# Feed-forward: weight places, the place of the last norm, and row additions moved from POOL to DVE

## The chip, the cores and the metric

The kernel runs on one core of a Trainium2 chip. The metric is the device time in microseconds of one execution, the median over runs. The engines named below: PE (TensorE, with its weight loads apart as PEld), DVE (VectorE), ACT (ScalarE), POOL (GpSimd) and SP (SyncE), whose queue issues all of this kernel's DMAs.

## What is computed

One layer of a streaming encoder for 1024 prompt tokens and 64 sample tokens with the same weights: attention with two groups of heads, cross-attention into a memory, then a feed-forward with a convolution. The change touches the end of the memory output projection and the feed-forward alone:

```python
def conv_ffn(h, prev, w_up, w_conv, b_conv, w_down):
    gu = h @ w_up
    gate, val = gu[..., :D_FF], gu[..., D_FF:]
    t = gate.shape[1]
    gp = jnp.concatenate([prev.astype(gate.dtype), gate], axis=1)
    conv = sum(gp[:, j:j + t] * w_conv[j] for j in range(CONV_W)) + b_conv
    y = (jax.nn.silu(conv) * val) @ w_down
    return y, gp[:, -(CONV_W - 1):]
...
xp = xp + mem_attend(rms_norm(xp, g_norm2[l]), mk, mv, w_mq[l], g_mq[l], w_mo[l])
f, conv_p = conv_ffn(rms_norm(xp, g_norm3[l]), zeros_prev, w_up[l], w_conv[l], b_conv[l], w_down[l])
xp = xp + f
```

D_MODEL is 1024 and D_FF 2816, all float32. The sample tokens go through the same code.

## The kernel before

Everything lies transposed: 128 features on the partitions, the 1088 tokens as columns, in two halves of H = 544 and four quarters of Q = 272. Each float32 operand of a matmul is split into a rounded part (`hi`, a cast on ACT) and the rest (`lo`, a subtraction on DVE), by `two_parts` (L1244 to L1246) or, with the norm's gain, `gained_parts` (L1248). A product of two such operands is three matmuls (`SPLIT`: hi hi, hi lo, lo hi).

**Order of the work.** The Python code traces the instructions in the order in which it runs. The framework's planner then gives each engine its queue: it simulates costs and can draw an instruction forward when it finds the engine free and the operands there. Each engine then runs its queue strictly in that order. SP's queue of DMAs is one of them.

**The end of the memory output.** The loop at L1409 makes the second half of the eight feature rows, in the order `ROWS` = 0, 4, 1, 5, 2, 6, 3, 7. `evict_mo` (L1230) adds the residual to the product on DVE (L1233), stores the row, squares it on ACT (L1241) and adds the square to `accs[1]` on POOL (L1242). `t_sums` (L1391 to L1404) makes the sums and differences of row blocks that the products of the up projection take on the right; it holds `vSh` and `vSl` as scratch.

**The up projection.** Both feed-forward matrix products are cut into 2 x 2 blocks and made with seven block products instead of eight, M1 to M7. Up: for each of 22 column tiles n (NF) the order is M1, M2, M6, M5, M7, M3, M4 (L1310). Each block product is 24 matmuls of 272 columns (`product`, L1371, the matmul at L1381) into one of four PSUM tiles `wides`. Its left operand is a quarter of the weights (n, 0 to 3), or a sum of quarters. `load_more` (L1332) loads quarters in order into the places of `raws`: two `kvraw`, then `vSh` and `vSl`, then three `raw` places of the stream of earlier weights. `prepare` (L1340) makes the sums on DVE (M6: L1348 and L1349; M7: L1351; M3: L1353) and splits the operand. The right operands are the parts that `t_sums` made, `t3_parts` (four splits, for M7) and `t4_parts` (four splits, for M4, in places that `accs[1]` and the sums held).

`norm3(z)` (L1288) sums `accs[z]` over the features with two matmuls of float32 (four in the trace, L1292) and makes 1/rms on DVE and ACT (L1295 to L1300). `rs[1]` is read by the gate's convolution (L1486), first after M3. `finish` (L1513) evicts a product; M1, M5 and M6 are kept aside on ACT (L1517). The loop around the change:

```python
for g, (n, what) in enumerate(order):
    hi_lo = ops.pop((n, what))
    w = product(n, what, ...)
    parts_.give(hi_lo)
    if g == 0:
        t3_parts()
        norm3(1)
        t4_parts()
    finish(n, what, w)
    while prepared < min(len(order), g + 1 + AHEAD):
        prepare(prepared)
        prepared += 1
```

**The down projection.** `DOWN` = M2, M1, M5, M3, M6, M7, M4 (L1549), each over 11 steps f, each step four row blocks m of six matmuls (L1678) into the same four PSUM tiles `ws`. `prepare_down` (L1595) makes the operands two steps ahead: sums on DVE (L1603, L1604 for M5; L1606, L1607 for M3; L1609 for M6; L1611, L1612 for M7; L1614 for M4) and two splits. At the last step of a product `finish_down` (L1626) adds each tile to the output row `y_of(k, z)` on DVE (through `add`, L1452). M5 and M6 start the tiles anew, so they must wait for that. M1's product belongs to four output blocks: ACT copies it to `p` (L1631), and its additions to two further rows (L1632, L1633) and the residual of the rows m + 4 (`residual`, L1639: a load of x into the one buffer `early_x` at L1642 and an addition at L1643) are put on the list `later`, of which one entry is taken after each step (L1689). All run on POOL.

Of the kernel before, what the change touches and what calls it, by code (L numbers as in the profile page):

```python
# [40 lines left out]
def hybrid_step(ctx: ExitStack, tc: tile.TileContext, i: dict, o: dict):  # L41
# [3 lines left out]
    def f32(ap):  # L45
        return ap.bitcast(F32)
# [1183 lines left out]
    def evict_mo(m, z, q0, q1, src, x):  # L1230

        x = x[:, q0:q1]
        dve.tensor_tensor(like(x, src), src, like(x, src), op=ALU.add)  # L1233
        nc.sync.dma_start(xd[m, :, z * H + q0:z * H + q1], x)
        if m == ROWS[0]:
            if accs[z] is None:
                accs[z] = long_row(("sq", "pth")[z])
            act.activation(accs[z][:, q0:q1], x, ACT.Square, scale=1.0 / 32)
        else:
            sq = long_row("qlo")[:, :q1 - q0]  # L1240
            act.activation(sq, x, ACT.Square, scale=1.0 / 32)  # L1241
            pool.tensor_tensor(accs[z][:, q0:q1], accs[z][:, q0:q1], sq, op=ALU.add)  # L1242

    def two_parts(hi, lo, t, e=None):  # L1244
        act.copy(hi, t)  # L1245
# [66 lines left out]
    def stream_place(tag):  # L1312
        return stream.pl.tile([P, 4, P], F32 if tag == "raw" else F32R, name=tag, bufs=3 if tag == "raw" else 4).rearrange("p k c -> p (k c)")

    def flat(tag):
        if tag in ("vSh", "vSl"):
            return pl.tile([P, 2, Q], F32R, name=tag).rearrange("p a b -> p (a b)")[:, :512]
        return tmp(tag, [P, 2, 256]).rearrange("p a b -> p (a b)")

    raws = Slots([lambda: f32(flat("kvraw"))] * 2 + [lambda x=x: f32(flat(x)) for x in ("vSh", "vSl")] + [lambda: stream_place("raw")] * 3)  # L1320
    parts_ = Slots([lambda x=x: (flat(x + "h"), flat(x + "l")) for x in ("kP", "vP", "kS")]
                   + [lambda: (stream_place("hi"), stream_place("lo"))] * 4)

# [210 lines left out]
    for g, (n, what) in enumerate(order):  # L1534
        hi_lo = ops.pop((n, what))
        w = product(n, what, lambda p, j: hi_lo[p][:, j * P:(j + 1) * P], 4, [right(what, j) for j in range(4)], True, True)
        parts_.give(hi_lo)
        if g == 0:
            t3_parts()
            norm3(1)  # L1540
            t4_parts()
        finish(n, what, w)
# [3 lines that stand above are left out]
# [9 lines left out]
    def y_of(m, z):  # L1555

        return tall[m + 8 * z]
# [68 lines left out]
    def finish_down(what, m, w):  # L1626
        k, z = {"M2": (m, 0), "M1": (m, 0), "M5": (m + 4, 1), "M3": (m, 1), "M6": (m, 1), "M7": (m + 4, 1), "M4": (m + 4, 0)}[what]
        dst = y_of(k, z)
        if what == "M1":
            p = y_of(m + 4, 0)  # L1630
            act.copy(halves(p), both(w))  # L1631
            later.extend([lambda: pool.tensor_tensor(y_of(m, 1), y_of(m, 1), p, op=ALU.add),  # L1632
                          lambda: pool.tensor_tensor(y_of(m + 4, 1), y_of(m + 4, 1), p, op=ALU.add)])  # L1633
            later.extend([lambda q=q: residual(m, q) for q in range(2)])
        add(dst, w, dst)
        if what in ("M1", "M6", "M7", "M4"):
            nc.sync.dma_start(o["yT"][k, :, z * H:z * H + H], dst)

    def residual(m, q):  # L1639

        c = slice(q * Q, q * Q + Q)
        nc.sync.dma_start(early_x[:, :Q], xd[m + 4, :, c])  # L1642
        pool.tensor_tensor(y_of(m + 4, 0)[:, c], y_of(m + 4, 0)[:, c], early_x[:, :Q], op=ALU.add)  # L1643

    later = []
    for f in range(NG):
        load_b("M2", f)
    load_a()
# [12 lines left out]
    for s, (what, f) in enumerate(steps):  # L1661
        if f < NG - 1:
            prepare_down(s + 2)
            load_a()
            nxt = DOWN.index(what) + 1
            if nxt < len(DOWN):
                load_b(DOWN[nxt], f)
                if f == NG - 2:
                    load_b(DOWN[nxt], NG - 1)
        if f == NG - 1:  # L1670
            continue
        for m in range(4):
            for x in ((s,) if f < NG - 2 else (s, s + 1)):
                la, ra = down_ops[x]
                first, final = steps[x][1] == 0, steps[x][1] == NG - 1
                for z in range(2):
                    for y, (p, b) in enumerate(SPLIT):
                        pe.matmul(ws[m][:, z, :Q], la[p][:, m * P:(m + 1) * P], ra[b][:, z * Q:z * Q + Q],  # L1678
                                  start=first and y == 0 and what in opening, stop=final and y == 2 and what in closing, skip_group_check=True)
            if f == NG - 2:  # L1680
                finish_down(what, m, ws[m])
        for x in ((s,) if f < NG - 2 else (s, s + 1)):
            la, ra = down_ops.pop(x)
            parts_.give(la)
            rights_.give(ra)
        if f == NG - 2:
            prepare_down(s + 3)
            load_a()
        if later:  # L1689
            later.pop(0)()  # L1690
    assert not later
    late_left.close()
    in_order(tc)

# [102 lines left out]
```

## Time and profile before

| | |
|---|---|
| Time, median of 3 runs | 1813.85 us (1813.5 to 1814.9) |
| The profiled execution's own time | 1811.59 us |
| Span of its trace, first to last instruction | 1809.8 us |
| Mean granted TensorE clock | 0.987 |
| Busy: PE, DVE, ACT, POOL | 1724.4, 1226.5, 929.6, 683.9 us |

The feed-forward runs from about 1091 us to the end: the up projection to 1562, the down projection to 1806. Busy times overlap, since the engines run beside each other. In a row of the timeline, what stands in brackets is the idle time of the engine before the instruction and what ended it; rows of like instructions are merged ("x2"), and since matmuls are pipelined, the busy times of neighbours overlap.

### The profile page before, as it was taken

Reading aid. Unit: us, or ns where it says so; the run is one execution under the profiler, and the core shown is the slowest. Engines: PE = TensorE matmul, PEld = TensorE weight load, DVE = VectorE, ACT = ScalarE, POOL = GpSimd, SP = SyncE. Lnnn points to the kernel's source line nnn. Section 1 sums busy time; section 2 is a strip of 40 time slices with the busy share of each in tenths; the row PEclk is TensorE's granted clock in tenths of the full one; section 3 lists DMA queues with packets and bytes.
Section 4 is the critical chain, followed back from the end, with each engine's and each line's share of the span. In section 5 each row is a group of like instructions: output and inputs, shape, how many; then the busy total and the mean of one; then the engine's idle time right before and its main releaser. Section 6 shows DMA issues by size and latency. Waiting matters only on the chain.

```text
span 1809.8 us, 34045 instructions
## 1 busy us (share of the span) xinstructions
PE 1724.4 (95%) x12412; PEld 1668.5 (92%) x12412; DVE 1226.5 (68%) x2693; ACT 929.6 (51%) x2042; POOL 683.9 (38%) x1042
## 2 busy tenths in 40 slices
PE   6899999999997898999999999999999999998999
PEld 5789999999997777999999998999999999998999
DVE  5777667677676788333444378877777777677974
ACT  5646666777676567334455455333333333433332
POOL 5746657878776454443343612000000001003000
PEclk9999999999998998999999999999999999999999
DMA  8312122122113767441111562222222222894222
GB/s 283 95 44 73 39 74 78 51 72 75 44 57 118 226 208 229 148 145 53 53 47 63 164 218 77 78 76 84 88 81 72 72 72 83 293 301 130 80 95 79
DMA packets 134104, 200.13 MB, mean 111 GB/s; under 512 B 20824, under 2 KB 73944, under 8 KB 133936
## 3 DMA queue, kind: packets, MB, share of 16 engines
q1 hardware_dynamic: 133936, 197.96, 34.5%
q8 instruction: 97, 1.59, 0.4%
q14 instruction: 71, 0.58, 0.1%
HBM read 155.61 MB, written 45.44 MB: 111 GB/s over the span
## 4 chain that ended last, share of the span: by engine, by line
PE 47%; DVE 4%; issue 1%; DMA 1%; POOL 1%; ACT 1%; SPq 0%; POOLq 0%; DVEq 0%; ACTq 0%
PE W L1381 25%; PE W L1678 9%; PE pj L869 7%; PE W L869 2%; PE S L1124 1%; PE tq L1160 1%; PE O L1160 1%; POOL lo L852 1%; DVE lo L1246 1%; DMA kvraw<-in_w_down_dram 0%; PE PT L1147 0%; DMA raw<-in_w_down_dram 0%; DVE f L1246 0%; PE O L1124 0%; DMA f<-x2d 0%
## 5 line engine op out<-in xcount | busy, mean ns | idle before, releaser
L272 PE MATMUL pj<-whi,xhi 128*128 128x384 f32 (+1 forms) x512 | 195.4, 382 | 7.9 <-ACT xhi L130 6.8
L272 PE MATMUL pj<-wlo,xhi 128*128 128x384 f32 (+1 forms) x512 | 177.1, 346 | 3.6 <-POOL wlo L123 3.3
L272 PE MATMUL pj<-whi,xlo 128*128 128x384 f32 (+1 forms) x512 | 175.4, 343 | 4.3 <-DVE xlo L131 4.3
L1487 POOL COPY s<-gp 128x2 f32<-128x2 f32 x22 | 15.8, 719 | 337.2 <-DVE gp L1486 337.2
L1678 PE MATMUL W<-f,hi 128*128 128x272 f32 x672 | 129.2, 289 | 7.7 <-DVE gp L1452 5.5
L458 ACT ACTIVATE s<-s,mx 128x640 f32<-128x640 f32 (+7 forms) x128 | 94.3, 736 | 80.0 <-DVE mx L456 78.3
L1381 PE MATMUL W<-h,hi 128*128 128x272 f32 x704 | 134.2, 288 | 0.7 <-ACT hi L1245 0.7
L495 DVE TENSOR_TENSOR ptl<-PT,pth 128x512 fp32r<-128x512 f32 (+2 forms) x192 | 99.5, 522 | 38.0 <-ACT pth L494 35.7
L1678 PEld LDWEIGHTS W<-f,hi 128*128 128x128 f32 x672 | 106.4, 190 | 8.8 <-DVE gp L1452 6.0
L1381 PEld LDWEIGHTS W<-h,hi 128*128 128x128 f32 x704 | 110.7, 188 | 0.9 <-ACT hi L1245 0.9
L224 POOL TENSOR_TENSOR r<-m,mhalf 128x4 f32<-128x4 f32 (+1 forms) x72 | 73.8, 1024 | 92.4 <-DVE m L223 79.0
L272 PEld LDWEIGHTS pj<-whi,xhi 128*128 128x128 f32 x512 | 99.7, 195 | 9.0 <-ACT xhi L130 6.8
L272 PEld LDWEIGHTS pj<-wlo,xhi 128*128 128x128 f32 x512 | 99.5, 194 | 5.7 <-POOL wlo L123 4.8
L494 ACT CAST pth<-PT 128x512 fp32r<-128x512 f32 (+2 forms) x192 | 84.8, 448 | 37.3 <-PE PT L493 35.7
L272 PEld LDWEIGHTS pj<-whi,xlo 128*128 128x128 f32 x512 | 97.9, 191 | 5.1 <-DVE xlo L131 5.1
L1381 PE MATMUL W<-h,lo 128*128 128x272 f32 x352 | 101.8, 289 | 0.0
L1678 PE MATMUL W<-f,lo 128*128 128x272 f32 x336 | 97.4, 290 | 0.0
L227 POOL TENSOR_SCALAR qk<-qkraw,r 128x128 f32<-128x128 f32 x256 | 92.7, 379 | 6.0
L493 PE MATMUL PT<-ident,s 128*128 128x128 f32 x528 | 90.2, 276 | 4.9 <-DVE ptl L495 3.8
L869 PE MATMUL pj<-a,hi 128*128 128x384 f32 (+1 forms) x352 | 89.5, 337 | 0.4 <-DVE qhi L1005 0.4
L453 PE MATMUL S<-kh,q 128*128 128x256 f32 (+1 forms) x304 | 76.8, 278 | 12.0 <-DVE mx L456 10.2
L1245 ACT CAST hi<-raw 128x512 fp32r<-128x512 f32 x55 | 34.2, 621 | 101.9 <-PE W L1381 55.3
(606 smaller groups left out, 6085.1 us busy)
## 6 DMA issues: line engine op xcount, KB each, us to landing
raw<-in_w_down_dram SPq DMA_DIRECT2D x45, 256.0 KB, 3.1
wraw<-in_w_dram SPq DMA_DIRECT2D x56, 192.0 KB, 2.4
raw<-in_w_up_dram SPq DMA_DIRECT2D x36, 256.0 KB, 2.7
h<-ad SPq DMA_DIRECT2D x32, 272.0 KB, 4.9
mwraw<-in_w_mkv_dram SPq DMA_DIRECT2D x16, 512.0 KB, 4.8
raw<-in_w_mo_dram SPq DMA_DIRECT2D x32, 256.0 KB, 3.2
kvraw<-in_w_down_dram SPq DMA_DIRECT2D x32, 256.0 KB, 3.1
ad<-t SPq DMA_DIRECT2D x22, 272.0 KB, 2.2
```

Of the source, the lines that this page charges most:

```text
L224: pool.tensor_tensor(r[:rows], m[:rows], mhalf[:rows, 0:4], op=ALU.pow)
L227: pool.tensor_scalar(qk[:rows, h], raw[:rows, h * 64:(h + 1) * 64].rearrange("p (o d) -> p o d", o=1).broadcast_to([rows, 2, 64]), r[:rows ...
L272: pe.matmul(pj[:, :nw], x2[a][:, k, t * P:(t + 1) * P], wt[k][b][:, :nw], start=n == 0, stop=n == 3 * KT - 1)
L453: pe.matmul(sp[:, a:a + (k1 - k0) * P], q, kk[:, h, src], start=m == 0, stop=m == 1)
L458: act.activation(s[:, :n], s[:, :n], ACT.Exp, bias=mx, scale=-1.0, accum_out=sm)
L493: pe.transpose(pt[:, b - ch[0]], self.s[j][:, (b - w0) * P:(b - w0 + 1) * P], ident)
L494: act.copy(hi[:, f:f + n, j], pt[:, f:f + n])
L495: dve.tensor_tensor(lo[:, f:f + n, j], pt[:, f:f + n], f32(hi[:, f:f + n, j]), op=ALU.subtract)
L869: pe.matmul(out()[:, :cn], w[a][:, k % 4], x[b][k][:, c0:c0 + cn], start=k == 0 and n == 0, stop=k == KT - 1 and n == 2)
L1160: pe.matmul(op[:, a0:a1], v[x][:, b, d * P:(d + 1) * P], self.p2[y][:, b, a0:a1], start=n == 0, stop=n == 5)
L1381: pe.matmul(w[:, z, :Q], a(p, j), rights[j][b][:, z * Q:z * Q + Q], start=fresh and begin and j == 0 and x == 0, stop=final and end and j ...
L1678: pe.matmul(ws[m][:, z, :Q], la[p][:, m * P:(m + 1) * P], ra[b][:, z * Q:z * Q + Q], start=first and y == 0 and what in opening, stop=fina ...
```

## The change

The last row's addition to `accs[1]` goes to DVE. `raws` gives out the three `raw` places before `vSh` and `vSl`. `norm3(1)` and `t4_parts()` are traced after the third product (g == 2, M6 of n = 0) instead of the first. In the down projection `later` becomes a list for each product: M1's eight row additions are taken in M6's steps and the eight residuals in M7's, one after each step, all on DVE.

```diff
@@ -1239,7 +1239,7 @@
         else:
             sq = long_row("qlo")[:, :q1 - q0]
             act.activation(sq, x, ACT.Square, scale=1.0 / 32)
-            pool.tensor_tensor(accs[z][:, q0:q1], accs[z][:, q0:q1], sq, op=ALU.add)
+            (dve if z and m == ROWS[-1] else pool).tensor_tensor(accs[z][:, q0:q1], accs[z][:, q0:q1], sq, op=ALU.add)
 
     def two_parts(hi, lo, t, e=None):
         act.copy(hi, t)
@@ -1317,7 +1317,7 @@
             return pl.tile([P, 2, Q], F32R, name=tag).rearrange("p a b -> p (a b)")[:, :512]
         return tmp(tag, [P, 2, 256]).rearrange("p a b -> p (a b)")
 
-    raws = Slots([lambda: f32(flat("kvraw"))] * 2 + [lambda x=x: f32(flat(x)) for x in ("vSh", "vSl")] + [lambda: stream_place("raw")] * 3)
+    raws = Slots([lambda: f32(flat("kvraw"))] * 2 + [lambda: stream_place("raw")] * 3 + [lambda x=x: f32(flat(x)) for x in ("vSh", "vSl")])
     parts_ = Slots([lambda x=x: (flat(x + "h"), flat(x + "l")) for x in ("kP", "vP", "kS")]
                    + [lambda: (stream_place("hi"), stream_place("lo"))] * 4)
 
@@ -1537,6 +1537,7 @@
         parts_.give(hi_lo)
         if g == 0:
             t3_parts()
+        if g == 2:
             norm3(1)
             t4_parts()
         finish(n, what, w)
@@ -1629,9 +1630,8 @@
         if what == "M1":
             p = y_of(m + 4, 0)
             act.copy(halves(p), both(w))
-            later.extend([lambda: pool.tensor_tensor(y_of(m, 1), y_of(m, 1), p, op=ALU.add),
-                          lambda: pool.tensor_tensor(y_of(m + 4, 1), y_of(m + 4, 1), p, op=ALU.add)])
-            later.extend([lambda q=q: residual(m, q) for q in range(2)])
+            later["M6"] += [lambda k=k: dve.tensor_tensor(y_of(k, 1), y_of(k, 1), p, op=ALU.add) for k in (m, m + 4)]
+            later["M7"] += [lambda q=q: residual(m, q) for q in range(2)]
         add(dst, w, dst)
         if what in ("M1", "M6", "M7", "M4"):
             nc.sync.dma_start(o["yT"][k, :, z * H:z * H + H], dst)
@@ -1640,9 +1640,9 @@
 
         c = slice(q * Q, q * Q + Q)
         nc.sync.dma_start(early_x[:, :Q], xd[m + 4, :, c])
-        pool.tensor_tensor(y_of(m + 4, 0)[:, c], y_of(m + 4, 0)[:, c], early_x[:, :Q], op=ALU.add)
-
-    later = []
+        dve.tensor_tensor(y_of(m + 4, 0)[:, c], y_of(m + 4, 0)[:, c], early_x[:, :Q], op=ALU.add)
+
+    later = {what: [] for what in DOWN}
     for f in range(NG):
         load_b("M2", f)
     load_a()
@@ -1686,9 +1686,9 @@
         if f == NG - 2:
             prepare_down(s + 3)
             load_a()
-        if later:
-            later.pop(0)()
-    assert not later
+        for _ in range(len(later[what]) and 1):
+            later[what].pop(0)()
+    assert not any(later.values())
     late_left.close()
     in_order(tc)
 
```

## Rows read from the trace of the kernel before

**Rows 1.** The page: engines' busy time, share, count; a DMA group.

```profile
PE 1724.4 (95%) x12412; PEld 1668.5 (92%) x12412; DVE 1226.5 (68%) x2693; ACT 929.6 (51%) x2042; POOL 683.9 (38%) x1042
...
kvraw<-in_w_down_dram SPq DMA_DIRECT2D x32, 256.0 KB, 3.1
```

**Rows 2.** Chain that ended last, whole run: start us, us, what.

```profile
1105.27 457.19 PE W L1381 x3640
...
1621.92 4.55 DMA kvraw<-in_w_down_dram
...
1640.03 26.45 PE W L1678 x197
...
1708.92 96.97 PE W L1678 x774
```

**Rows 3.** Windows: us, busy (count) by engine, PEclk, DMA share, GB/s.

```profile
1105.27:1108.30 3.03, 3.03 (x13) 3.03 (x14) 3.03 (x6) 0.00 (x0) 0.00 (x0) 0.51 0.00 0
...
1620.00:1630.00 10.00, 8.16 (x65) 7.94 (x65) 7.87 (x10) 3.81 (x7) 3.32 (x2) 1.00 0.90 288
...
1630.40:1640.03 9.63, 4.11 (x20) 3.65 (x19) 9.63 (x11) 1.99 (x4) 9.63 (x7) 0.82 0.48 160
```

**Rows 4.** Chain that ended last, asked from 1040 to 1130 us.

```profile
1105.27 24.77 PE W L1381 x185
```

**Rows 5.** Timeline of PE, start of the up projection: start, duration, what.

```profile
1095.14 1.18 PE L1292 MATMUL W<-pth,ones 128*128 128x272 f32 x4 [0.35 <-POOL pth L1242]
...
1100.33 0.49 PE L1381 MATMUL W<-h,kPh 128*128 128x272 f32 x2 [0.98 <-ACT f L1245]
```

**Rows 6.** Timeline of SP's queue, loads of the first up weights.

```profile
1080.14 0.33 SPq L1336 DMA_DIRECT2D raw<-in_w_up_dram  x1
...
1098.35 0.33 SPq L1336 DMA_DIRECT2D vSl<-in_w_up_dram  x1
```

**Rows 7.** Timeline of DVE, start of the up projection.

```profile
1091.82 0.72 DVE L1233 TENSOR_TENSOR qhi<-W,qhi 128x544 f32<-128x544 f32 x1 [2.49 <-PE W L869]
...
1093.79 1.88 DVE L1246 TENSOR_TENSOR t<-f,t 128x544 fp32r<-128x544 f32 x1
...
1101.37 0.68 DVE L1348 TENSOR_TENSOR vSh<-vSh,vSl 128x512 f32<-128x512 f32 x1
...
1115.69 0.43 DVE L1473 TENSOR_TENSOR gp<-W,qlo 128x272 f32<-128x272 f32 x1
```

**Rows 8.** Timeline of POOL, the last addition to accs[1].

```profile
1093.43 1.66 POOL L1242 TENSOR_TENSOR pth<-pth,qlo 128x544 f32<-128x544 f32 x1 [2.61 <-ACT qlo L1241]
```

**Rows 9.** Timeline of PE, M1 to M5 of the down projection.

```profile
1625.07 0.39 PE L1678 MATMUL W<-f,hi 128*128 128x272 f32 x1 [1.84 <-DVE f L1246]
...
1634.21 0.82 PE L1678 MATMUL W<-f,hi 128*128 128x272 f32 x2 [3.72 <-DVE gp L1452]
```

**Rows 10.** Timeline of DVE, down projection, M1 to M5, and M6.

```profile
1627.23 1.75 DVE L1607 TENSOR_TENSOR raw<-raw,qlo 128x512 f32<-128x512 f32 x1
...
1639.27 0.71 DVE L1452 TENSOR_TENSOR gp<-W,gp 128x544 f32<-128x544 f32 x1
...
1721.90 1.98 DVE L1614 TENSOR_TENSOR h<-h,f 128x544 f32<-128x544 f32 x3
```

**Rows 11.** Lines L1632 (x4, ns), L1643 (a wait), L1642 (landing).

```profile
L1632 POOL TENSOR_TENSOR f<-f,t x4: 1624/1688/1802, 1626.7 to 1638.7; 128x544 f32<-128x544 f32 x4
...
  DMA x<-x2d: 11.4, 5
...
DMA to landing us min/median/max: 2.0/2.1/2.1
```

**Rows 12.** Timeline of SP's queue, M1 to M5 of the down projection.

```profile
1627.22 0.33 SPq L1591 DMA_DIRECT2D kvraw<-in_w_down_dram  x1
```

**Rows 13.** Windows in M6 and M7 of the down projection.

```profile
1720.00:1730.00 10.00, 10.00 (x83) 10.00 (x82) 10.00 (x17) 3.52 (x7) 0.00 (x0) 1.00 0.01 2
...
1760.00:1770.00 10.00, 10.00 (x82) 10.00 (x81) 4.66 (x8) 3.50 (x6) 0.00 (x0) 1.00 0.32 98
```

## The prediction

> **What bounds the kernel now.** The page comes first: TensorE (PE) is busy 95% of the span [rows 1], so the question is which of its few holes this change touches. The chain that ended last shows where PE is not the bound [rows 2]: at 1091.8 us, when the last row of the memory output product is done, the chain leaves PE for DVE and returns only at 1105.3 us. From there one piece of 3640 matmuls takes 457.19 us: 0.1256 us for each, the price of a matmul here, undisturbed. A second such place ends at 1640.03 us. From 1708.92 us on 774 matmuls run in 96.97 us, 0.1253 each: the last three products (M6, M7, M4) have no hole at all.
>
> **First hole, start of the up projection.** Until 1105.27 us PE does from 1091.49 us M1 and M2 of n = 0 (48 matmuls), norm3(1)'s four (started over about 0.9 us) and four pairs that the planner drew ahead: 56 x 0.1256 + 0.9 = 7.9 us of work in 13.8 us, so 5.9 us are lost. Behind it the clock is down: the granted clock is 0.51, the lower level of 1.2 GHz, for 3 us [rows 3], and 185 matmuls take 24.77 us [rows 4] where 23.2 would do: 1.5 us more. Together 7.4 us. PE waits in this order [rows 5]: for POOL's last addition to accs[1] (norm3(1), 0.35), then with the pairs for ACT and DVE (0.98 before the first), until M6's left operand is there. That operand is late for two reasons. Its weights: quarter (0,3) goes to vSl, which t_sums still uses, so that its load is issued at 1098.35 us, while a load into a `raw` place went out at 1080.14 [rows 6]. And DVE's queue: DVE idles 2.49 us before 1091.82 us, then works without a gap; the first addition for M6 (L1348) starts at 1101.37 us, behind t_sums, the t3 and t4 parts and norm3(1) [rows 7]. One subtraction takes 1.88 us there, against 0.68 for L1348's, while POOL adds [rows 7, 8].
>
> **Second hole, M1 to M5 of the down projection.** M5 opens the same PSUM tiles that M1 closes, so its matmuls wait for DVE to add each tile out. PE stands 3.72 us for the first [rows 9], and again for the last, to 1640.03 us. M1's matmuls end about 1630.4 us; until 1640.03 us 18 matmuls run (2.3 us of work): 7.3 us lost, and the next 197 take 26.45 us [rows 2] instead of 24.7: 1.7 us at the low clock, which is 0.82 on average over the hole [rows 3]. Together 9.0 us. DVE is busy all this time, with instructions of 0.7 us that take up to 1.75 [rows 10]: POOL is adding M1's rows then, at 1.69 us each [rows 11], and the two alternate.
>
> **The change part by part.** Durations are from the profiled execution, 1811.59 us with a span of 1809.8; the median of the runs is 1813.85, 2.3 us more, and the sum is taken off the median. DVE's instructions overlap a little: three of 544 columns take 1.98 us [rows 10], so one of them counts 0.64 us in a queue, and one of 512 columns 0.60.
>
> *Places of the weights.* No load is added or removed. Quarters (0,2), (0,3), (1,0) go to the three `raw` places, whose loads stand at the same points of SP's queue, one of them at 1080.14 [rows 6]; (1,1) and (1,2) take vSh and vSl, and are not due before M2 of n = 1. A load of this size lands in about 3 us [rows 1], so a21 and a22 are there by about 1086 us, and L1348, L1349 and the subtraction for kSl (3 x 0.62 = 1.9 us) fit DVE's 2.49 us of idle time before 1091.82 [rows 7]. If the planner does not put them there, they cost 1.9 us behind t_sums.
>
> *norm3(1) and the t4 parts later.* Four DVE instructions of norm3(1) and four of t4 (8 x 0.64 = 5.1 us), with two and four ACT instructions, move behind M6's matmuls. rs[1] is first read after the sixth product, the t4 parts in the seventh. PE still pays its 0.9 us. With M6's parts early, PE runs M1 to 1094.5, M2 to 1097.5, M6 to 1100.5. DVE from 1091.82: eviction, addition to accs[1], six instructions of t_sums, four t3 parts (12 x 0.64 = 7.7 us, to 1099.5), then M5's subtraction (1100.1, due 1100.5), an eviction, M7's two (1101.9, due 1103.5), M3's two (1103.1, due 1106.5), norm3(1) and t4 (1108.2), M4's (1108.8, due about 1110.5). Cover holds, with 0.4 us at the tightest place.
>
> *Last addition to accs[1] on DVE.* POOL loses one addition of 1.66 us [rows 8], DVE gains one of 0.64 and loses the 1.2 us that it stood behind POOL. The new wait is DVE's for ACT's Square; behind it in DVE's queue stand t_sums' instructions, and for them PE. The Square needs only DVE's eviction, so between 0 (the planner puts L1400 ahead) and about 0.7 (one ACT instruction of this shape, as DVE's own). I keep 1.0 us of the hole for this and the tight place: **gain 6.4**, bounds 3.7 (the rival below) and 7.4.
>
> *Row additions in M6, on DVE.* POOL's eight (four of 1.69 us, four of the same shape) leave M1 and M5 [rows 11]; eight of 0.64 come onto DVE in M6, 5.1 us. At the hole, with the same queue and nothing slowed, the ten instructions from 1627.23 to the last eviction take 4 x 0.64 + 6 x 0.60, hence 6.2 us: it ends about 1634.1 instead of 1640.0 [rows 10]. One of the ten needs a weight load issued at 1627.22 [rows 12]; landing in 3.1 to 4.55 us [rows 1, 2], it adds 0 to 1.5. I take 0.8: 1634.9, that is 5.1 us. PE then idles in pieces below the 1.84 us that it stood at 1625 [rows 9], which the clock, at 1.00 from 1620 to 1630 [rows 3], went through without a fall, so the 1.7 us come back too: **gain 6.8**, bounds 4.4 and 9.0. In M6 itself DVE is 10.00 of 10 busy at 1720 us [rows 13], but of that 1.98 us in one row alone are three subtractions for M4 [rows 10], due 40 us later: they move back and are the cover. Without it, the 5.1 us are on the path.
>
> *Residuals in M7, on DVE.* Eight additions of 272 columns, about 0.43 us each as a like one [rows 7], 3.4 us, in a stage where DVE is 4.66 of 10 busy [rows 13]. Their x loads move from SP's queue in M5 to M7, behind M6's outputs and among M4's weight loads, which run several steps ahead: nothing, or a step's delay of one load. DVE now waits for them where POOL did, 11.4 us in five waits [rows 11]; between 0 and 2.4 us a step (landing 2.1, issue 0.3), taken at 0, since the step is 3.0 us and must hold only two subtractions (1.3) and the addition.
>
> The sum is 6.4 + 6.8 = 13.2 us: 1800.7.
>
> A rule that speaks against it: the Trainium skill (Perfetto Trace Analysis, Optimizing Scalar/DVE Operations) says that with DVE saturated, offloading work to GPSIMD may make sense, and adds that it might not help, since the two share a read port. By its first half this change, which loads DVE by 8.5 us more in M6 and M7, would lose that: 1822. The rows above bear out its second half.
>
> **The rivals.** *DVE's queue stays ahead of M6 in the up projection* (0.17, with the next one): the planner, which already draws instructions out of the order of the program (M1 of n = 1 stands before M6 of n = 0 [rows 5]), leaves M6's three behind t_sums. Then only what stood before them goes: three of norm3(1), two t4 parts and 1.2 us of slowing, less 0.64: 3.7 us. Gain 3.7 + 6.8: 1803.4. *Weights bind M5:* DVE's early M3 work, not POOL, holds the evictions; if three such loads of 3 to 4.5 us stand in front, the second hole shrinks by 2 only: 13.2 - 4.8, hence 1805.5. Both at once: 1808.2. Against it: DVE's rows there are long, not idle.
>
> *The residuals' waits stand in DVE's queue* (0.06, slower): each waits for a load that can start only after the addition before it, since early_x is one buffer. If M7's own preparations are not done ahead (four instructions, 2.6 us of a 3.0 us step), each of eight steps grows by 2.4: 19.5 us against 13.2, hence 1820. It decides where DVE enters M7 with no lead. For it speaks the wait that POOL shows; against it DVE's idle half in M7 [rows 13].
>
> *No more than moved* (0.09): the planner restores about the old order, or both holes reopen one product later, at M5 of the up projection (cover 0.4 us) and at M6: 1811 to 1816.
>
> **How the numbers follow.** The forecast has 0.68 and spans 1796 to 1805, by the bounds of its two terms. One hole staying in part reaches to 1810. A measurement of this kernel can tell about 0.2%, 3.6 us. Faster: 0.68 + 0.17 = 0.85; same 0.09; slower 0.06. The range 1796 to 1810 leaves out the last two cases and little else.
>
> **What would show it.** Right: no idle PE over 1 us between 1091 and 1112 us, kSl written before 1092, granted clock 1.00 there; M5's first matmul within 1 us of M1's last, no POOL instruction in the down projection, and DVE's 128x544 additions at 0.72 throughout. Wrong: kSl still behind t_sums; DVE idle on `x` loads in M7 with PE waiting; evictions behind weight waits at M5; or PE idle in M6, now without a hole.

## The result and the profile after

| | before | after |
|---|---|---|
| Median of 6 runs | 1813.67 us (1811.36 to 1815.09) | 1801.51 us (1797.74 to 1803.87) |
| Profiled execution, its span | 1811.59, 1809.8 us | 1798.58, 1796.5 us |
| Up projection starts at | 1091.6 us | 1089.9 us |
| Length of the up projection | 470.7 us | 465.7 us |
| Length of the down projection | 243.3 us | 236.7 us |

The ratio is 0.9931, with a 95% interval of 0.9917 to 0.9945: 12.2 us less between the medians. The lengths are read from the trace: from the first matmul of L1381 to the first of L1678, and from there to the start of the last one, each to 0.1 us. They are the finer measure here, and not without noise: among the profiled executions below, stages that an edit leaves alone differ by 0.6 us up (465.6 to 466.2) and 1.7 us down (235.8 to 237.5). The two stages that the change touches are 5.0 and 6.6 us shorter. Of the 13.3 us between the two spans, 1.7 us lie ahead of the up projection; the changed kernel's own two profiles start it at 1089.9 and 1091.6 us, those of its variants below at 1086.0 to 1094.1, so nothing of this size can be put down to the change.

The page after, the line of the engines (as [rows 1]):

```profile
PE 1718.8 (96%) x12412; PEld 1663.7 (93%) x12412; DVE 1225.0 (68%) x2710; ACT 930.5 (52%) x2042; POOL 662.8 (37%) x1025
```

17 instructions went from POOL to DVE, and DVE's busy time fell all the same, from 1226.5 to 1225.0 us: what it took over is paid for by the instructions that no longer run beside POOL. By their durations in the trace of before, the DVE instructions that overlap POOL's sixteen additions and residuals are 10.0 us longer in all than at 0.72 us (544 columns) or 0.69 us (512) each; on DVE the sixteen take 9.6 us (8 x 0.73 and 8 x 0.47).

The chain that ended last (start us, us, what):

```profile
1108.65 447.07 PE W L1381 x3570
...
1628.90 24.90 PE W L1678 x197
...
1695.52 97.11 PE W L1678 x774
```

Against [rows 2]: the long piece of the up projection now costs 0.1252 us for each matmul instead of 0.1256, since the half-speed stretch at its head is gone, and the 197 matmuls behind M1 to M5 take 24.90 us instead of 26.45.

What PE waited for in the two projections (us in total, times, longest):

```profile
PE W L1678 <- DVE f L1246: 3.1, 1, 3.1
PE W L1381 <- ACT qlo L1517: 1.4, 1, 1.4
PE W L1678 <- DVE f L1452: 0.4, 1, 0.4
PE W L1381 <- ACT qhi L1517: 0.2, 1, 0.2
```

Four waits of 5.1 us are left. None of them is for M1's evictions (`gp L1452`), the 3.72 us of [rows 9]. The two long ones are new or longer, and the experiments turn on them.

Windows (us, busy and count of PE, PEld, DVE, ACT, POOL, then PEclk, DMA share, GB/s):

```profile
1085.00:1115.00 30.00, 28.43 (x221) 27.84 (x220) 29.55 (x52) 17.50 (x30) 4.98 (x9) 1.00 0.22 75
...
1618.50:1628.90 10.40, 9.14 (x60) 8.93 (x60) 9.32 (x16) 4.59 (x8) 0.00 (x0) 0.84 0.90 305
...
1700.00:1720.00 20.00, 20.00 (x163) 20.00 (x162) 20.00 (x35) 7.63 (x14) 0.00 (x0) 1.00 0.17 49
1720.00:1740.00 20.00, 20.00 (x160) 19.91 (x160) 19.95 (x34) 8.09 (x14) 0.00 (x0) 1.00 0.47 157
```

The granted clock stays at 1.00 where it was 0.51 [rows 3]. From 1700 to 1740 us, in M6 and M7, DVE is full and PE has no hole. But at the end of M1 the clock falls, which it did not do there before.

The up projection's start, on DVE and then on PE (timeline: start, duration, what):

```profile
1083.77 0.68 DVE L1348 TENSOR_TENSOR raw<-raw 128x512 f32<-128x512 f32 x1
...
1086.45 0.68 DVE L1246 TENSOR_TENSOR kSl<-kvraw,kSh 128x512 fp32r<-128x512 f32 x1
...
1091.96 0.71 DVE L1233 TENSOR_TENSOR qhi<-W,qhi 128x544 f32<-128x544 f32 x1
...
1107.14 0.73 DVE L1300 SCALAR_TENSOR_TENSOR sq<-qlo 128x544 f32<-128x544 f32 x1
```

```profile
1096.31 0.52 PE L1381 MATMUL W<-f,kSh 128*128 128x272 f32 x2 [0.20 <-ACT qhi L1517]
...
1099.42 1.08 PE L1292 MATMUL W<-pth,ones 128*128 128x272 f32 x4
...
1108.65 0.52 PE L1381 MATMUL W<-h,hi 128*128 128x272 f32 x2 [1.37 <-ACT qlo L1517]
```

M6's operand is ready at 1087.1 us: L1348 stands 17.6 us earlier than in [rows 7] (15.9 against the start of the up projection). DVE has no gap here, and the last eviction of the memory output (L1233) comes 1.9 us after PE's last matmul for it, which ended at 1090.1 us; before, it followed at once. M6 opens at 1096.31 after 0.20 us, and norm3(1) waits for nothing. The new wait is the last row: this matmul adds onto the PSUM tile in which M5's result still lies, and ACT copies that result out only here:

```profile
1107.98 0.61 ACT L1517 COPY qlo<-W 128x544 f32<-128x544 f32 x1 [2.74 <-DVE sq L1300]
```

The copy goes into the row `qlo`, and norm3(1) uses that row as scratch until L1300, at 1107.14.

The moved additions and residuals (min/median/max ns, first and last start; M6's matmuls begin at 1692.7 us, M7's at 1726.4):

```profile
L1633 DVE TENSOR_TENSOR f<-f,t x8: 731/736/743, 1679.0 to 1699.1; 128x544 f32<-128x544 f32 x8
```

```profile
L1643 DVE TENSOR_TENSOR t<-t,x x8: 440/469/472, 1705.9 to 1731.0; 128x272 f32<-128x272 f32 x8
```

The program has them in M6 and M7, but the planner drew them forward by up to 14 and 20 us: additions run from M3 on, and seven of the eight residuals start in M6. On POOL an addition took 1.69 us [rows 11]. DVE waits for no `x` load, where POOL waited 11.4 us.

### The profile page after: what moved, and what is told of

It is laid out like the page before. It is cut to its first block, busy times and chain, and to the rows that moved or that the text cites. A ratio compares the mean times of both kernels' runs of the same rounds, so it can differ in the third digit from the quotient of the medians.

```text
span 1796.5 us, 34030 instructions
## 1 busy us (share of the span) xinstructions
PE 1718.8 (96%) x12412; PEld 1663.7 (93%) x12412; DVE 1225.0 (68%) x2710; ACT 930.5 (52%) x2042; POOL 662.8 (37%) x1025
## 4 chain that ended last, share of the span: by engine, by line
PE 46%; DVE 3%; DMA 2%; issue 2%; POOL 1%; ACT 1%; SPq 0%; POOLq 0%; ACTq 0%; DVEq 0%
PE W L1381 25%; PE W L1678 9%; PE pj L869 7%; PE W L869 2%; DMA raw<-in_w_down_dram 1%; PE S L1124 1%; PE tq L1160 1%; PE O L1160 1%; POOL lo L852 1%; DVE lo L1246 0%; PE PT L1147 0%; DVE f L1246 0%; PE O L1124 0%; DMA kvraw<-in_w_down_dram 0%; DMA h<-ad 0%
## 5 line engine op out<-in xcount | busy, mean ns | idle before, releaser
L1381 PE MATMUL W<-h,hi 128*128 128x272 f32 x704 | 134.4, 288 | 1.4 <-ACT qlo L1517 1.4
L1678 PE MATMUL W<-f,hi 128*128 128x272 f32 x672 | 128.3, 288 | 3.2 <-DVE f L1246 3.1
L1381 PEld LDWEIGHTS W<-h,hi 128*128 128x128 f32 x704 | 110.8, 188 | 1.7 <-ACT qlo L1517 1.6
L1678 PEld LDWEIGHTS W<-f,hi 128*128 128x128 f32 x672 | 106.0, 189 | 3.8 <-DVE f L1246 3.3
L1381 PE MATMUL W<-h,lo 128*128 128x272 f32 x352 | 101.8, 289 | 0.0
L1245 ACT CAST hi<-raw 128x512 fp32r<-128x512 f32 x68 | 42.2, 621 | 108.8 <-PE W L1381 58.2
L1678 PE MATMUL W<-f,lo 128*128 128x272 f32 x336 | 97.1, 289 | 0.0
```

The source lines that it names most:

```text
L1381: pe.matmul(w[:, z, :Q], a(p, j), rights[j][b][:, z * Q:z * Q + Q], start=fresh and begin and j == 0 and x == 0, stop=final and end and j ...
```

## The experiments

Every edit is made to the changed kernel; "changed" below is 465.7 us up and 236.7 us down. Medians are of 4 to 10 runs. The kernel before had medians of 1811.27 to 1813.67 us in the four sets of runs, so medians from different sets can differ by about 2 us without a cause. The edits are shown shortened. They shift line numbers: the sum for M5 that was L1603 before is L1604 in the changed kernel and L1611 in the last variant, and the down projection's matmul is L1678 to L1687.

### Up projection: which part brought the 5.0 us

**The buffers in their old order.**

```diff
-raws = kvraw x2, raw x3, vSh, vSl
+raws = kvraw x2, vSh, vSl, raw x3
```

> The changed kernel, with vSh and vSl again ahead of the three raw places. Theory (the late weights of M6 were a cause of their own): quarter (0,3) is loaded again only after t_sums, at about 1097 us, lands about 3 us later, and kSl is written at about 1103 us, two later than M2's end by 5; PE stands 4 to 6 us before M6, the clock falls behind it, and nearly the whole gain of the up projection (5.1 us from its first to its last matmul) is lost: up projection 470 to 472 us long instead of 465.8, time 1805.5 to 1807.5. Rival (DVE's queue was the bound, and the norm's place has freed it): the length grows by 2 us or less, time below 1803.7.

Measured: up 468.5, down 236.2 us, median 1803.14. By the length 2.8 us are lost, less than the theory asked and more than the rival allowed; the median lies within what the rival gave. M6's weights came late, as said, but the planner put ten of M5's matmuls ahead of M6, so PE had work.

**The norm in its old place** (behind the first product).

```diff
-        if g == 2:
             norm3(1)
             t4_parts()
```

> The changed kernel, with norm3(1) and t4_parts again after the first product. Theory (the weights come first, the norm's place is worth little once M6's parts are made ahead): PE waits 1 to 2 us for accs[1] before norm3(1), the wait of 1.4 us for the qlo row before M7 or M5 goes, and the up projection is within 1.5 us of 465.8; time 1800.5 to 1803. Rival (eight DVE instructions, 5.1 us, stand ahead of what PE needs): it grows by 3 to 5 us, time 1804.5 to 1806.5.

Measured: up 465.6, down 237.5 us, median 1799.06. The length is as the theory had it, the median 1.4 us below its range. With the weights early, the norm's place is worth nothing: it waits 1.55 us for its sum of squares, and the wait for `qlo` is gone in exchange.

**Both at once**, the last addition left on DVE.

> Edit: the weights' buffers in their old order and the last norm in its old place, the addition of the norm's last square left on DVE. With old buffers alone the up projection took 468.5 us, with the old norm place alone 465.6 us, with neither 465.7 us. Theory (the two parts are one mechanism, as the prediction priced them together: the norm stands ahead of M6's preparation on DVE only if that preparation is late): together they cost more than the sum of both, the up projection takes 469.3 to 470.7 us, and M6's opening waits return at 1100 to 1106. Rival (the norm's place is worth nothing in either case): 468.0 to 469.0 us.

Measured: up 470.4 us, down 236.8, median 1805.21. The theory holds. PE's waits there (timeline):

```profile
1100.90 0.49 PE L1381 MATMUL W<-h,kPh 128*128 128x272 f32 x2 [1.03 <-DVE qlo L1295]
...
1103.04 0.82 PE L1381 MATMUL W<-h,hi 128*128 128x272 f32 x2 [1.65 <-ACT hi L1245]
...
1105.15 0.59 PE L1381 MATMUL W<-f,kSl 128*128 128x272 f32 x1 [0.39 <-DVE kSl L1246]
```

The last one is M6's first matmul with its low part, at 1105 us again. Of the four combinations the up projection takes:

| | norm behind M1 | norm behind M6 |
|---|---|---|
| old order of buffers | 470.4 | 468.5 |
| new order of buffers | 465.6 | 465.7 |

The order of the buffers brings 4.8 us alone, the norm's place 1.9 alone, and both together no more than the first.

**The last addition back on POOL.**

```diff
-(dve if z and m == ROWS[-1] else pool).tensor_tensor(accs[z]...
+pool.tensor_tensor(accs[z]...
```

> The changed kernel, with the last addition to accs[1] on POOL again. Theory (it is off the path now): one DVE subtraction takes 1.2 us longer, accs[1] is ready 1 us later, and both are covered, since norm3(1) stands behind M6; time within 1 us of the changed kernel. Rival (DVE has no slack between t_sums and M7): 1.2 to 2 us longer.

Measured: up 466.7, down 236.6 us, median 1802.14. POOL's addition costs about 1 us, in the wait for `qlo`, which grows from 1.37 to 2.46 us: norm3(1) ends later, so the copy does. The theory had it covered, and it is not.

**The norm one product earlier** (behind M2), to test that wait.

```diff
-        if g == 2:
+        if g == 1:
             norm3(1)
+        if g == 2:
             t4_parts()
```

> Edit: the last norm is traced behind M2 (one product earlier than in the changed kernel), the parts of the fourth sum stay behind M6. Theory: the 1.37 us wait of the matmul at 1108.65 comes from ACT's copy of M5, which needs the row qlo that the norm holds until 1107.14; with the norm one product earlier that row is free before the copy, the wait goes and the up projection takes 464.0 to 464.8 us (465.7). Rival: the norm's matmuls then wait for the sum of squares on DVE (as the 1.55 us in the run with the norm in its old place), and the wait is only exchanged: 465.4 to 466 us.

Measured: up 464.0 us, median 1795.31, ratio 0.9908 (0.9887 to 0.9929). The theory holds. The whole list of PE's waits in both projections, and ACT's copy:

```profile
PE W L1679 <- DVE f L1246: 3.2, 1, 3.2
```

```profile
1101.59 0.61 ACT L1517 COPY qlo<-W 128x544 f32<-128x544 f32 x1 [3.26 <-DVE sq L1300]
```

The copy still follows L1300 at once, but against the start of the up projection both come 2.5 us earlier, ahead of PE. Of the 6.2 us by which this median lies below 1801.51, only 1.7 can be put down to the edit: in this profiled execution the up projection started at 1086.0 us, and in the last but one run below, with the same edit, at 1092.9.

### Down projection: engine or place

The changed kernel moves the row additions to another engine and to another place at once. Three runs fill in the other combinations.

**Additions and residuals on POOL in their old places** (one after each step from the end of M1 on).

```diff
-later["M6"] += [lambda k=k: dve.tensor_tensor(y_of(k, 1), ...) for k in (m, m + 4)]
-later["M7"] += [lambda q=q: residual(m, q) for q in range(2)]
+later.extend([lambda: pool.tensor_tensor(y_of(m, 1), ...), lambda: pool.tensor_tensor(y_of(m + 4, 1), ...)])
+later.extend([lambda q=q: residual(m, q) for q in range(2)])
```

> The changed kernel, with the list of row additions and residuals as before, on POOL after each step from M1's last on. Theory (POOL's additions slowed DVE's evictions): the hole of about 7 us before M5's last opening matmul comes back, with DVE instructions of 1.2 to 1.9 us, and the down projection is 6 to 9 us longer than 236.9; time 1807.5 to 1810.5. Rival (the weight loads bind there): 2 us or less, time below 1803.7.

Measured: up 465.8, down 247.1 us, median 1806.17. The hole is back, 10.4 us in the profiled execution and 4.7 between the medians: more than the theory's 6 to 9 us by the length, less than it by the median. DVE at the end of M1, and POOL and PE beside it (timelines):

```profile
1621.98 1.75 DVE L1604 TENSOR_TENSOR kSh<-kSh,kvraw 128x512 f32<-128x512 f32 x1 [1.83 <-DMA kvraw<-in_w_down_dram]
1623.66 1.87 DVE L1608 TENSOR_TENSOR raw<-raw,qlo 128x512 f32<-128x512 f32 x1
...
1629.78 0.71 DVE L1452 TENSOR_TENSOR gp<-W,gp 128x544 f32<-128x544 f32 x1
```

```profile
1629.27 1.78 POOL L1633 TENSOR_TENSOR f<-f,t 128x544 f32<-128x544 f32 x1
```

```profile
1630.54 0.82 PE L1679 MATMUL W<-f,hi 128*128 128x272 f32 x2 [4.11 <-DVE gp L1452]
```

From 1621.98 to 1630.41 us the DVE instructions with both operands in SBUF take 1.2 to 1.9 us beside POOL instead of 0.69 to 0.72. The eviction at 1629.78, which reads one operand from PSUM, runs in the middle of one of POOL's additions and takes its 0.71.

**On DVE in their old places.**

```diff
-later["M6"] += ...
-later["M7"] += ...
+later.extend([lambda: dve.tensor_tensor(y_of(m, 1), ...), lambda: dve.tensor_tensor(y_of(m + 4, 1), ...)])
+later.extend([lambda q=q: residual(m, q) for q in range(2)])
```

> Edit: the eight additions and eight residual additions stay on DVE, but go back to their old places (one after each step from the end of M1 on, through M5 into M3). Theory (the engine is what counts: POOL's additions slow DVE's two-input operations from about 0.7 to 1.75 us): on DVE they cost 8 x 0.73 + 8 x 0.47 = 9.6 us spread over M5 and the start of M3, where DVE has 7 us of 20 free in 1640 to 1660; the waits of M5's first matmuls on L1452 stay under 1 us, and the down projection takes 236.5 to 239 us (236.7 in the changed kernel). Rival (the place is what counts: M1's end is late whatever engine adds): the first additions stand ahead of M5's evictions and preparations on DVE, the half-speed stretch behind M1's end comes back, 242 to 247 us.

Measured: down 235.8 us, median 1800.52. The engine counts; the rival would have given 242 or more. The planner drew these additions forward too, to 1622.4 us and on, about where POOL's ran in the run before (from 1621.8).

**On POOL in their new places.**

```diff
-later["M6"] += [lambda k=k: dve.tensor_tensor(...
+later["M6"] += [lambda k=k: pool.tensor_tensor(...
-dve.tensor_tensor(y_of(m + 4, 0)[:, c], ...
+pool.tensor_tensor(y_of(m + 4, 0)[:, c], ...
```

> Edit: the additions and residual additions go to POOL, in the changed kernel's places (M6 and M7). Theory (engine): DVE is full from 1680 to 1740; it is relieved of 9.6 us but its operations run slower beside some 13 us of POOL's additions and 6 us of its residuals, so the gain is given back: down projection 236 to 239 us, with DVE operations of 1.2 to 1.9 us in M6. Rival (place): no matmul of M6 hangs on them and DVE is relieved, so it is as good or better, 235 to 236.7 us, and DVE is no longer full from 1700 to 1740.

Measured: down 246.8 us, median 1809.76. The direction is the theory's, but its size is far off: relieved of 9.6 us of its own work, DVE kept PE waiting. (The places are the program's; POOL ran four of the additions at 1659.7 to 1667.5 us and four at 1696.2 to 1705.3.) The timelines of DVE and POOL, the window (columns as above) and PE's waits from 1655 to 1745 us:

```profile
1699.71 1.63 DVE L1246 TENSOR_TENSOR lo<-ptl,hi 128x512 fp32r<-128x512 f32 x1
...
1704.25 1.63 DVE L1246 TENSOR_TENSOR lo<-sq,hi 128x512 fp32r<-128x512 f32 x1
```

```profile
1699.11 3.43 POOL L1633 TENSOR_TENSOR f<-f,t 128x544 f32<-128x544 f32 x2
...
1703.71 1.62 POOL L1633 TENSOR_TENSOR f<-f,t 128x544 f32<-128x544 f32 x1
```

```profile
1700.00:1720.00 20.00, 18.21 (x132) 17.76 (x132) 20.00 (x24) 6.24 (x11) 9.56 (x9) 0.91 0.16 43
```

```profile
PE W L1678 <- DVE f L1246: 3.0, 2, 2.1
PE W L1678 <- DVE f L1452: 1.8, 1, 1.8
```

From 1700 to 1720 us DVE is as full as in the changed kernel, but with 24 instructions instead of 35, and PE does 132 matmuls instead of 163. Against the changed kernel, 4.4 of the 4.8 us of waits are new (M3 to M6 had 0.4), and the clock, 0.91 from 1700 to 1740, takes another 3.6; they are most of the 10.1. The four combinations, down projection and median:

| | places in M1, M5, M3 | places in M6, M7 |
|---|---|---|
| POOL | 247.1 (1806.17) | 246.8 (1809.76) |
| DVE | 235.8 (1800.52) | 236.7 (1801.51) |

The engine is worth about 10 us in the profiled executions and 6 to 8 between the medians, the place nothing on DVE. DVE's own load is about the same either way: the DVE instructions that overlap POOL's sixteen are 9.1 us (old places) and 9.4 us (new places) longer in all, counted as above, where the sixteen take 9.6 us on DVE. So what changes is which of DVE's instructions come late. The planner can order the additions in DVE's queue, and POOL's slowing falls on whatever runs beside it: that would explain the 10 us, but it is argued, not shown.

### The wait that was left at the end of M1

**The residual rows loaded later**, to test whether the DMA traffic makes it.

```diff
-            if m < 4 or z:
+            if m < 4 and not z:
                 nc.sync.dma_start(y_of(m, z), ...)
...
+        if what == "M5" and f < 8:
+            nc.sync.dma_start(y_of((f + 4) % 8, 1), xd[(f + 4) % 8, :, H:N])
```

> Edit: the eight loads of the right halves of the residual rows (272 KB each, needed from the end of M5 on) go from ahead of the down projection into M5's first eight steps. Theory: the 3.10 us wait at the end of M1 and the half-speed stretch behind it (1.45 us) come from M5's weights, whose DMAs share 0.85 to 0.95 busy engines with those 2.2 MB (about 7 us at 300 GB/s); without them the weights land in time and the down projection takes 232 to 234 us (236.7). Rival: the weights are late because a buffer comes free late, not because of the traffic: the wait stays at 2.5 to 3.1 us and the down projection at 236 to 237 us. Second rival: the loads in M5 get in the way there, and a wait for DMA appears in M5: 237 us or more.

Measured: down 238.7 us, median 1802.55. A miss for the theory, and no test of it: the planner drew the eight loads forward to 1593.5 to 1624.0 us, into M1, and the DMA engines stayed 0.83 to 0.93 busy from 1590 to 1630 us. The run is instructive all the same. The wait at M1's end fell to 0.87 us and the clock stayed up there, but two waits for evictions came in its place, 3.5 us in all: one at M1's opening, for M2's last eviction, with the clock at 0.83 from 1590 to 1600 us, and one at M5's opening, for M1's last. DVE and PE (timelines):

```profile
1591.73 0.72 DVE L1605 TENSOR_TENSOR h<-h,h 128x544 f32<-128x544 f32 x1 [1.81 <-DMA h<-ad]
...
1592.97 0.72 DVE L1452 TENSOR_TENSOR gp<-W,gp 128x544 f32<-128x544 f32 x1
...
1624.20 0.69 DVE L1607 TENSOR_TENSOR qlo<-qlo,kvraw 128x512 f32<-128x512 f32 x1 [1.17 <-DMA kvraw<-in_w_down_dram]
```

```profile
1593.74 0.82 PE L1680 MATMUL W<-qhi,hi 128*128 128x272 f32 x2 [2.76 <-DVE gp L1452]
...
1630.57 0.52 PE L1680 MATMUL W<-f,hi 128*128 128x272 f32 x2 [0.73 <-DVE gp L1452]
```

L1605 is a subtraction for M5, 35 us ahead of M5's first matmul; it stands in front of M2's last eviction and waits for its load. L1607 is a sum for M3, 37 us ahead of M3's first matmul; it stands in front of M1's evictions and waits for its weights. That led back to the changed kernel's own trace, DVE ahead of the 3.10 us:

```profile
1616.29 0.69 DVE L1604 TENSOR_TENSOR sq<-sq,kvraw 128x512 f32<-128x512 f32 x1 [1.23 <-DMA kvraw<-in_w_down_dram]
1617.04 0.69 DVE L1604 TENSOR_TENSOR vPl<-vPl,kvraw 128x512 f32<-128x512 f32 x1
1617.65 0.68 DVE L1604 TENSOR_TENSOR kSl<-kSl,raw 128x512 f32<-128x512 f32 x1
1618.25 0.68 DVE L1246 TENSOR_TENSOR lo<-qlo,hi 128x512 fp32r<-128x512 f32 x1
1618.86 0.72 DVE L1246 TENSOR_TENSOR f<-h,f 128x544 fp32r<-128x544 f32 x1
```

The cast on ACT and the matmul that waited:

```profile
1613.11 0.64 ACT L1245 CAST f<-h 128x544 fp32r<-128x544 f32 x1
```

```profile
1619.63 0.60 PE L1678 MATMUL W<-f,hi 128*128 128x272 f32 x1 [3.10 <-DVE f L1246]
```

The cast for the subtraction at 1618.86 was done at 1613.75. The subtraction stood 5 us in DVE's queue behind three additions for steps 4, 8 and 10 of M5 (the rows `sq`, `vPl`, `kSl` of `sums`), the first of which waited for its weights. In all twelve kernels in which the additions are not held, the one before included, DVE stood for loads at the additions of steps 4 and 8 just ahead of this wait, for 0.8 to 1.7 us together. The 14 matmuls from 1619.63 to 1622.96 then took 3.33 us, where 1.75 would do at 0.125 each: 1.6 us of clock.

**The additions held back**, with the norm one product earlier.

```diff
             dve.tensor_tensor(S, S, a["A22"], op=ALU.add)
+            after_step(s - 2)    # order on DVE alone: behind the last instruction of prepare_down(s - 2)
```

> Edit: the norm one product earlier, as in the run before, and M5's eleven additions S += A22 held behind the last preparation of the step two before their own on DVE's queue (an order on one engine, no semaphore); in the changed kernel the tracer's planner put them up to nine steps ahead. Theory: the 3.10 us at 1619.63 are not a late weight of M5's second step (its copy on ACT was done by 1613.8) but three additions for steps 4, 6 and 10 of M5 that stand ahead of it on DVE and wait for their weights until 1616.29; held back, they leave no wait, no half-speed stretch follows, and the down projection takes 231.5 to 233.5 us (236.7, and 235.8 in two runs with a wait of 1.6 and 3.2); with the up projection at 464.0 us the whole is 1789 to 1793 us. Rival: the weights of M5 as a whole are late (DMA engines 0.9 busy from 1540 to 1630), and since their buffers now come free later, M5's own steps wait: one or more waits on M5's operands of 1 to 4 us in the first 25 us of M5 and a down projection of 235 to 240 us, 1794 to 1799 us.

Measured: up 464.5, down 230.7 us, median 1794.23 (1792.48 to 1795.06), ratio 0.9899 (0.9887 to 0.9912). The theory's mechanism holds, and the down projection is shorter than it asked; the rival's late weights do not show. The median lies above the theory's 1789 to 1793 us, which were counted from the run before, whose up projection started 6.9 us earlier. (The expectation takes the middle one of the three additions for step 6's; by the list of `sums` it is step 8's.) All of PE's waits in both projections, the chain, and the additions on DVE:

```profile
PE W L1381 <- ACT qlo L1517: 0.5, 1, 0.5
```

```profile
1557.54 230.89 PE W L1687 x1848
```

```profile
1612.81 0.69 DVE L1611 TENSOR_TENSOR qlo<-qlo,raw 128x512 f32<-128x512 f32 x1
...
1615.86 0.68 DVE L1611 TENSOR_TENSOR qlo<-qlo,raw 128x512 f32<-128x512 f32 x1
...
1618.84 0.69 DVE L1611 TENSOR_TENSOR pth<-pth,raw 128x512 f32<-128x512 f32 x1
```

The down projection is one piece: its 1848 matmuls run without a wait, at 0.1249 us each. The additions come about one in 3 us, just ahead of their use, and none waits for a load, though the DMA engines are 0.97 busy from 1608 to 1618 us: traffic alone makes no wait here. The run with the norm alone took 235.8 us down, so holding the additions is worth 5.1 us against it and 6.3 against the kernel below. The medians do not separate these two variants: 1794.23 and 1795.31 us, with intervals that overlap.

**The changed kernel beside it**, on the same chip.

> The changed kernel itself beside the two others, so that each stands against it on one chip. Expected: up projection 465.7 us and down projection 235.8 to 236.7 us, 1799 to 1802 us. If its up projection starts at 1086 to 1087 us instead of 1089.9, as in the run with the norm one product earlier, then that earlier start belongs to the run and not to the edit.

Measured: up 466.2, down 237.0 us, median 1799.0 (1794.41 to 1801.09), ratio 0.9918 (0.9904 to 0.9932), with the waits of 3.2 and 1.4 us in their places and the up projection starting at 1091.6 us. The held version is 4.8 us below it between the medians, and 6.7 between the profiled executions: 1.7 up and 6.3 down, less 1.3 that its up projection started later.

## Why the prediction was right, and where its steps were off

The sum was 13.2 us; the medians differ by 12.2 and the two stages by 11.6. That the terms come so near is in part luck, as the steps show. The likeliest case came about; neither DVE's late queue nor the residuals' waits did. Of the rival in which a hole reopens one product later there is a trace, the 1.37 us at 1108.65, though its cause was not DVE's queue. Two slips of the working change nothing: the bounds of the two terms give 1797.5 to 1805.8 us, not 1796 to 1805, and eight steps of 2.4 us are 19.2, not 19.5. Its steps one by one. (The sign asked for no idle PE over 1 us from 1091 to 1112: one such wait was there; kSl before 1092, clock 1.00, no POOL instruction in the down projection and 0.72 to 0.74 us for the additions were as said.)

**Places of the weights: right.** The planner put L1348, L1349 and the subtraction for kSl ahead of t_sums' end (1083.77 to 1087.1). They did not simply fit the 2.49 us of idle time: with the early sums for M7 and M3 beside them, DVE reached the last eviction 1.9 us late, and no matmul waited for that. The place alone is worth 4.8 us, by the run without it.

**norm3(1) and t4 parts later: the step that failed in the up projection.** "Cover holds, with 0.4 us at the tightest place" counted DVE's queue and nothing else. It left out the row: norm3(1) takes `qlo` as scratch, and `finish` copies M5's result into that same row. Moved behind M6, the norm held the row for 1.37 us too long. The gain was 5.0 us where 6.4 was forecast, and the difference is this wait; with the norm behind M2 the projection takes 464.0 us, a gain of 6.7. The step also earned nothing by itself once the weights were early (465.6 and 465.7 us).

**Last addition on DVE: right in direction, and no cost.** I kept 1.0 us of the hole for it. Put back on POOL, it costs 1.0 us more, through the wait for `qlo`. With buffers and norm as before it brings 0.3 us at most (470.4 us against 470.7), which is within the noise.

**Row additions in M6: size right by luck, from two errors that cancel.** 6.6 us against 6.8. The eviction waits went almost wholly, where I had left 2.2 of the 9.0 us. But "PE then idles in pieces below the 1.84 us that it stood at 1625" was wrong: that wait for `f L1246` [rows 9], which I took as fixed, became 3.10 us, and the clock fell behind it for 1.6. The trace of before shows the cause, and I read past it: a relative of the rival "weights bind M5", early instructions that wait for weights, but for M5's late steps where the rival had M3's. One of them there, on DVE:

```profile
1622.48 0.69 DVE L1603 TENSOR_TENSOR vPl<-vPl,kvraw 128x512 f32<-128x512 f32 x1 [0.59 <-DMA kvraw<-in_w_down_dram]
```

Held back, they free the whole of the wait. Why it was 1.84 us before and 3.10 after is not settled. Over the kernels in which the additions are not held it was 0.9 to 3.5 us, with the DMA engines 0.84 to 0.92 busy in the 10 us ahead of it; what sets the landing of those loads stays open, since the one run meant to try it did not keep its loads out of M1.

**The cover in M6, residuals in M7: right, with the residuals drawn forward into M6.** DVE is full from 1700 to 1740 us, M4's early subtractions moved back as the cover (the last is 187 us into the stage, 170 before), no matmul of M6 or M7 waits but for the 0.40 us at M6's opening, and no residual waits for its load.

**POOL or DVE.** The prediction said that POOL's additions, not the additions' place, make the hole, and the four combinations show it. The Trainium skill (Perfetto Trace Analysis, Optimizing Scalar/DVE Operations) allows offloading from a saturated DVE to GPSIMD, with the warning that the shared read port may undo it. Here the warning decides: on POOL in the same places the kernel takes 1809.76 us, 8.3 more.

## What to carry to other kernels

Before an instruction sequence is moved behind other work, list the scratch rows it holds and who takes them next; a free engine is not enough. On an engine that runs its queue in order, an instruction drawn far ahead of its use is harmless only if its operand is there: when a short preparation is late although its own input is ready, look for such an instruction in front of it, and hold it back to a step or two before its use. POOL additions beside a full DVE relieved nothing here: they cost DVE about as much (9.1 to 10.0 us) as they take on DVE itself (9.6), and the delay fell on whichever instructions ran beside them.

## What was not expected of the hardware

DVE's slowing beside POOL hung on where its operands lay. Twelve evictions from PSUM that ran wholly beside POOL's additions (the kernel before and the two runs with additions on POOL) took 0.71 to 0.72 us. Most instructions with both operands in SBUF took 1.0 to 1.9 us there; a few, such as some that started together with a POOL addition, kept their 0.7.

The length of a stop does not tell by itself whether PE's granted clock falls behind it. It fell behind the stop of 3.10 us, and behind one of 1.79 us in M6 of the run with POOL in the new places. It stayed at 1.00 through the stop of 1.84 us [rows 3, 9], and through one of 2.81 us at the end of M1 with the norm in its old place. The windows of the second and the fourth:

```profile
1702.00:1706.50 4.50, 4.47 (x22) 4.25 (x23) 4.50 (x5) 1.17 (x2) 3.33 (x3) 0.62 0.13 35
```

```profile
1620.00:1630.00 10.00, 7.18 (x57) 6.97 (x56) 7.68 (x12) 3.81 (x7) 0.00 (x0) 1.00 0.89 303
```

And with nothing held up, 1848 matmuls in a row keep 0.1249 us each over 231 us, with the clock at 1.00 from 1557.4 to 1788.4 us.
